# Splitting the two loads that follow stores in a DMA-fed batched matmul (a·bᵀ, fp32 in and out)

## Chip, core and metric

The kernel runs on one core of a Trainium2 chip. The metric is the device time of one launch in microseconds, given as the median of several runs. Shares and durations come from one further execution that the hardware profiler recorded.

## What is computed

```python
batch, m, k, n = 16, 512, 512, 512
a = randn(batch, m, k)   # float32
b = randn(batch, n, k)   # float32
out = matmul(a, b.transpose(0, 2, 1)).astype(float32)   # out[e] = a[e] @ b[e].T
```

Every operand is 16 x 512 x 512 float32, 16.78 MB. Two of them are read and one is written, 50.33 MB in all.

## The kernel before

**Work.** The sixteen batches are taken as eight pairs, `u` = 0 to 7. A load brings one operand of one pair: two batches, 1024 rows of 512 floats, 2 MB. It is laid over the 128 partitions so that each partition holds eight consecutive rows, which is one run of 16 KB in HBM for each partition. Loads are counted by `n_ld`: even ones are `a`, odd ones `b`, and load `n_ld` belongs to pair `n_ld // 2`. A store writes one batch of the output, 1 MB, four rows and so a run of 8 KB for each partition; stores are counted by `n_st`.

**Engines.** VectorE (DVE) casts each load into two bf16 halves (`ha`, `wa` or `hb`, `wb`, lines 167 to 175). TensorE (PE) transposes them (line 247) into PSUM tile `tp`. ScalarE (ACT) brings the transposed `a` back (`ta`, line 206) and VectorE the transposed `b` (`tb`, line 187). TensorE multiplies (line 266) into `ps`, and ScalarE copies the product into the output buffer `ob` (line 224).

**Buffers.** There are `NL` = 7 load slots and `NO` = 7 output slots. Load `n_ld` may be issued once the cast of load `n_ld` - 7 has gone far enough (`s_cd`). A store may be issued once its batch is in `ob` (`s_out`).

**Queue.** All loads, and all stores but the first, are issued by SyncE (SP) into one DMA queue, in an order written out by hand; the waits above are taken by SP in that order:

```python
ORDER = "LLLLLLLLLSSSLLLLLSSSLLSSSSSSSSS"
```

So nine loads (0 to 8) come first, then stores 1 to 3, loads 9 to 13, stores 4 to 6, loads 14 and 15, and stores 7 to 15. Store 0 is issued by GpSimd (POOL, line 135) into a queue of its own. The first two loads are already issued as two transfers of 1 MB each (lines 103 and 106), four rows and 8 KB for each partition, so that VectorE can begin early; all others are one transfer of 2 MB (line 110). Stores are issued on line 115.

**Who tells the engines that a load is there.** GpSimd walks the same `ORDER`. For each load it waits on the semaphore of the load's slot, `s_ld[slot]`, which grows by 16 when a transfer has landed, and then adds to `s_go`, on which VectorE waits. For the loads that are one transfer it adds 2 to `s_go` at once.

Of the kernel before, what the change touches and what calls it, by code (L numbers as in the profile page):

```python
# [10 lines left out]
def kernel(  # L11
# [6 lines left out]
    nc = tc.nc  # L18
# [3 lines left out]
    J = M // P  # L22
# [6 lines left out]
    NL = 7  # L29
# [5 lines left out]
    def sbuf(name, shape, dtype):  # L35
        return ctx.enter_context(nc.sbuf_tensor(name, shape, dtype))

    def sem(name):
        return tc.alloc_semaphore(name)

    with tc.tile_critical(no_gpsimd_drain=True):  # L41
        ident = sbuf("ident", [P, P], bf16)
        one = sbuf("one", [P, 1], f32)
        ld = sbuf("ld", [P, NL, 2 * J, K], f32)
# [10 lines left out]
        s_ld = [sem(f"s_ld{i}") for i in range(NL)]  # L55
        s_second = [sem(f"s_second{i}") for i in range(2)]
# [3 lines left out]
        def landed(n):  # L60
            return 16 * (n // NO + (n % NO > 0))
# [27 lines left out]

        n_ld, n_st = 0, 1
        for what in ORDER:
            if what == "L":
                u, slot = n_ld // 2, n_ld % NL
                src = (a if n_ld % 2 == 0 else b)[2 * u:2 * u + 2].rearrange(
                    "e (p j) k -> (e p) j k", j=2 * J
                )
                if n_ld >= NL:

                    nc.sync.wait_ge(s_cd, n_ld - NL + 2)
                if n_ld < 2:
                    nc.sync.dma_start(
                        ld[:, slot, :J, :], src[:, :J, :]
                    ).then_inc(s_ld[slot], 16)
                    nc.sync.dma_start(
                        ld[:, slot, J:, :], src[:, J:, :]
                    ).then_inc(s_second[slot], 16)
                else:
                    nc.sync.dma_start(ld[:, slot], src).then_inc(s_ld[slot], 16)  # L110
                n_ld += 1
            else:
                slot = n_st % NO
                nc.sync.wait_ge(s_out, n_st + 1)
                nc.sync.dma_start(
                    out[n_st].rearrange("(p j) n -> p j n", j=J), ob[:, slot]
                ).then_inc(s_st[slot], 16)
                n_st += 1
        for n in range(batch - NO, batch - 1):
            nc.sync.wait_ge(s_st[n % NO], landed(n))  # L120


        n_ld, n_st = 0, 1
        for what in ORDER:
            if what == "L":
                got = nc.gpsimd.wait_ge(s_ld[n_ld % NL], 16 * (n_ld // NL + 1))
                if n_ld < 2:
                    got.then_inc(s_go, 1)
                    nc.gpsimd.wait_ge(s_second[n_ld], 16).then_inc(s_go, 1)
                else:  # L130
                    got.then_inc(s_go, 2)
                n_ld += 1
                if n_ld == 4:
                    nc.gpsimd.wait_ge(s_out, 1)
                    nc.gpsimd.dma_start(  # L135
                        out[0].rearrange("(p j) n -> p j n", j=J), ob[:, 0]
                    ).then_inc(s_first, 16)
                elif n_ld == NL:
                    nc.gpsimd.wait_ge(s_first, 16).then_inc(s_of, 1)
            else:  # L140
                if n_st < batch - NO:
                    nc.gpsimd.wait_ge(
                        s_st[n_st % NO], landed(n_st)
                    ).then_inc(s_of, 1)
                n_st += 1
# [12 lines left out]
        with nc.Fori(0, pairs, engines=[dve]) as u:  # L158
            for x, (h, w, s_c, s_w) in enumerate(
                ((ha, wa, s_ca, s_wa), (hb, wb, s_cb, s_wb))  # L160
            ):
                src = ld[:, bass.ds((u * 2 + x) % NL, 1)].rearrange("p o j k -> p (o j) k")
# [148 lines left out]
```

## Time and profile before

| | |
|---|---|
| median of 5 runs | 126.8 us (126.28 to 127.26) |
| the profiled execution's own time | 127.23 us |
| its span, first to last instruction | 125.4 us |
| TensorE, VectorE, ScalarE busy | 73%, 56%, 54% of the span |
| DMA queue of SP (q1) | 49.29 MB, 93.8% of the 16 DMA engines' span |
| DMA queue of GpSimd (q0) | 1.05 MB, 2.0% |
| moved in all | 50.33 MB, 401 GB/s over the span |
| granted TensorE clock, mean | 0.953 |

A transfer runs on 16 DMA engines at once, each of which serves 8 of the 128 partitions; for each partition of a transfer there is one packet (16 KB for a whole load, 8 KB for a store), and each engine ends a transfer with a packet of 4 bytes that moves the semaphore. "Landing" is the time from the issue of a transfer to the last of the 16 semaphore steps. In the slices of the page each digit is a tenth of busy time in a fortieth of the span (3.14 us), and the row GB/s is what the DMA engines moved in it. The DMA share can read slightly over 1 in a short window, since a packet counts in the window where it begins.

### The profile page before, as it was taken

Reading aid. Unit: us, or ns where it says so; the run is one execution under the profiler, and the core shown is the slowest. Engines: PE = TensorE matmul, PEld = TensorE weight load, DVE = VectorE, ACT = ScalarE, POOL = GpSimd, SP = SyncE. Lnnn points to the kernel's source line nnn. Section 1 sums busy time; section 2 is a strip of 40 time slices with the busy share of each in tenths; the row PEclk is TensorE's granted clock in tenths of the full one; section 3 lists DMA queues with packets and bytes.
Section 4 is the critical chain, followed back from the end, with each engine's and each line's share of the span. In section 5 each row is a group of like instructions: output and inputs, shape, how many; then the busy total and the mean of one; then the engine's idle time right before and its main releaser. Section 6 shows DMA issues by size and latency. Waiting matters only on the chain. (4 is left out here: it accounts for less than half of the span.)

```text
span 125.4 us, 2407 instructions
## 1 busy us (share of the span) xinstructions
PE 91.6 (73%) x768; PEld 56.7 (45%) x768; DVE 70.1 (56%) x112; ACT 68.2 (54%) x130; POOL 1.7 (1%) x7
## 2 busy tenths in 40 slices
PE   0005299998998999899608999894989998994000
PEld 0005294477347646744408645741476457441000
DVE  0055679658867884792058894789058569400000
ACT  4005135589459567955820666934596669655000
POOL 2000000030000000000000000000000000000000
PEclk9999999999999999999995999999999999999655
DMA  4999999999999999999999999999999999999950
GB/s 94 400 431 444 444 418 423 428 423 381 408 449 423 418 428 421 423 434 431 402 423 423 444 439 428 413 418 428 434 418 449 389 428 421 434 423 423 428 251 10
DMA packets 4896, 50.33 MB, mean 401 GB/s; under 512 B 544, under 2 KB 544, under 8 KB 544
## 3 DMA queue, kind: packets, MB, share of 16 engines
q1 hardware_dynamic: 4752, 49.29, 93.8%
q0 software_dynamic: 144, 1.05, 2.0%
HBM read 33.55 MB, written 16.78 MB: 401 GB/s over the span
## 5 line engine op out<-in xcount | busy, mean ns | idle before, releaser
L266 PE MATMUL ps<-tb,ta 128*128 128x512 bf16 x256 | 58.0, 379 | 2.2 <-PEq L148 1.8
L224 ACT COPY ob<-ps 128x512 f32 x64 | 34.6, 588 | 27.2 <-PE ps L266 23.4
L206 ACT COPY ta<-tp 128x512 bf16<-128x512 bf16 x64 | 32.9, 604 | 18.8 <-PE tp L247 18.8
L266 PEld LDWEIGHTS ps<-tb,ta 128*128 128x128 bf16 x256 | 24.0, 97 | 32.7 <-issue 5.7
L247 PE MATMUL tp<-ident,ha 128*128 128x128 bf16 x256 | 19.9, 234 | 12.6 <-PEq L148 12.6
L247 PEld LDWEIGHTS tp<-ident,ha 128*128 128x128 bf16 x256 | 17.3, 106 | 15.9 <-issue 14.2
L247 PE MATMUL tp<-ident,hb 128*128 128x128 bf16 x256 | 18.5, 230 | 8.0 <-PEq L148 7.8
L187 DVE COPY tb<-tp 128x1024 bf16<-128x1024 bf16 x32 | 21.3, 685 | 4.2 <-DVEq L148 4.1
L247 PEld LDWEIGHTS tp<-ident,hb 128*128 128x128 bf16 x256 | 16.3, 104 | 8.7 <-issue 8.7
L167 DVE CAST hb<-ld 128x1024 bf16 x8 | 5.5, 694 | 13.9 <-DVEq L148 13.9
L182 DVE COPY ha<-wa 128x2048 bf16<-128x2048 bf16 x8 | 5.6, 694 | 10.9 <-DVEq L148 10.6
L167 DVE CAST ha<-ld 128x1024 bf16 x8 | 5.5, 687 | 6.5 <-DVEq L148 6.5
L172 DVE CAST hb<-ld 128x1024 bf16 x8 | 5.5, 687 | 1.1 <-DVEq L148 1.1
L172 DVE CAST ha<-ld 128x1024 bf16 x8 | 5.5, 688 | 1.0 <-DVEq L148 1.0
L186 DVE COPY hb<-wb 128x2048 bf16<-128x2048 bf16 x8 | 5.5, 686 | 0.5 <-DVEq L148 0.5
L175 DVE CAST wa<-ld 128x1024 bf16 x8 | 5.5, 686 | 0.0
L170 DVE CAST wb<-ld 128x1024 bf16 x8 | 5.5, 686 | 0.0
L170 DVE CAST wa<-ld 128x1024 bf16 x8 | 5.5, 686 | 0.0
L175 DVE CAST wb<-ld 128x1024 bf16 x8 | 5.5, 686 | 0.0
L197 ACT ACT_TABLE_LOAD x1 | 1.3, 1283 | 1.1 <-SPq L41 1.1
L135 POOL DMA_DIRECT2D out_dram<-ob x1 | 1.1, 1053 | 23.6 <-ACT ob L224 23.6
L83 POOL TENSOR_SCALAR_AFFINE_SELECT ident<-ident 128x128 bf16<-128x128 bf16 x1 | 0.3, 284 | 0.2 <-POOL ident L81 0.2
(6 smaller groups left out, 0.8 us busy)
## 6 DMA issues: line engine op xcount, KB each, us to landing
out_dram<-ob SPq DMA_DIRECT2D x15, 1024.0 KB, 22.2
ld<-in_a_dram SPq DMA_DIRECT2D x7, 2048.0 KB, 29.7
ld<-in_b_dram SPq DMA_DIRECT2D x7, 2048.0 KB, 33.6
ld<-in_a_dram SPq DMA_DIRECT2D x2, 1024.0 KB, 6.2
ld<-in_b_dram SPq DMA_DIRECT2D x2, 1024.0 KB, 10.2
out_dram<-ob POOLq DMA_DIRECT2D x1, 1024.0 KB, 13.1
```

The costliest lines, as they stand in the source:

```text
L167: nc.vector.tensor_copy(out=h[:, :J, :], in_=src[:, :J, :HK]).then_inc(s_cd, 1)
L170: nc.vector.tensor_copy(out=w[:, :J, :], in_=src[:, :J, HK:])
L172: nc.vector.tensor_copy(out=h[:, J:, :], in_=src[:, J:, :HK]).then_inc(s_c, 1)
L175: nc.vector.tensor_copy(out=w[:, J:, :], in_=src[:, J:, HK:]).then_inc(s_w, 1)
L182: nc.vector.tensor_copy(out=ha[:], in_=wa[:]).then_inc(s_ca, 1)
L186: nc.vector.tensor_copy(out=hb[:], in_=wb[:]).then_inc(s_cb, 1)
L187: nc.vector.tensor_copy(out=tb[:, ko, :], in_=tp[:, 2 + ko % 2].rearrange("k j p -> k (j p)"),).then_inc(s_eb, 1)
L197: nc.scalar.copy(out=one[:], in_=nc.const_aps.tensor(1.0, (P, 1), f32))
L206: c = nc.scalar.copy(out=ta[:, ko, e * J * P:(e + 1) * J * P].rearrange("k (j p h) -> k j p h", j=J, h=2), in_=tp[:, ko % 2, :, e * HP:(e ...
L224: c = nc.scalar.copy(out=dst[:, j, :].rearrange("m (p j) -> m p j", j=2 * J), in_=ps[:, j, :].rearrange("m (j p) -> m p j", j=2 * J),)
L247: t = nc.tensor.transpose(tp[:, 2 * x + g, j, :], h[:, j, g * P:(g + 1) * P], ident[:])
L266: t = nc.tensor.matmul(ps[:, j, :], ta[:, ko, (e * J + j) * P:(e * J + j + 1) * P], tb[:, ko, :].rearrange("k (j p) -> k j p", j=2 * J)[:, ...
```

## The change

A load that comes right after a store in `ORDER` is issued as two transfers instead of one: first the first four rows of each partition (a run of 8 KB), then the last four. By `ORDER` these are load 9 (`b` of pair 4, slot 2) and load 14 (`a` of pair 7, slot 0). Both transfers step the same semaphore `s_ld[slot]`; a list `count` holds what the semaphore must reach for each load, and GpSimd waits for that, so it still waits for the whole load. The data lands in the same places. On SP there are 33 rows of instructions instead of 31: two more DMA issues and nothing else. On the other engines the instructions and their order are the same; only line numbers move by 7.

```diff
+        parts = [0] * NL
+        count = []
+        last = None
         n_ld, n_st = 0, 1
         for what in ORDER:
             if what == "L":
...
-                if n_ld < 2:
+                if n_ld < 2 or last == "S":
                     nc.sync.dma_start(
                         ld[:, slot, :J, :], src[:, :J, :]
                     ).then_inc(s_ld[slot], 16)
-                    nc.sync.dma_start(
-                        ld[:, slot, J:, :], src[:, J:, :]
-                    ).then_inc(s_second[slot], 16)
+                    nc.sync.dma_start(ld[:, slot, J:, :], src[:, J:, :]).then_inc(
+                        s_second[slot] if n_ld < 2 else s_ld[slot], 16
+                    )
+                    parts[slot] += 1 if n_ld < 2 else 2
                 else:
                     nc.sync.dma_start(ld[:, slot], src).then_inc(s_ld[slot], 16)
+                    parts[slot] += 1
+                count.append(16 * parts[slot])
                 n_ld += 1
...
                 n_st += 1
+            last = what
...
-                got = nc.gpsimd.wait_ge(s_ld[n_ld % NL], 16 * (n_ld // NL + 1))
+                got = nc.gpsimd.wait_ge(s_ld[n_ld % NL], count[n_ld])
```

## Prediction

> **What bounds the kernel now.** I read the slices of the page first, for whether any resource is full the whole time.
>
> ```profile
> PE   0005299998998999899608999894989998994000
> ACT  4005135589459567955820666934596669655000
> DMA  4999999999999999999999999999999999999950
> GB/s 94 400 431 444 444 418 423 428 423 381 408 449 423 418 428 421 423 434 431 402 423 423 444 439 428 413 418 428 434 418 449 389 428 421 434 423 423 428 251 10
> q1 hardware_dynamic: 4752, 49.29, 93.8%
> ```
>
> The DMA row is at 9 from the second slice to the last but two, while PE and ACT have stopped two slices before. The 16 DMA engines are the bound: 50.33 MB at some 425 GB/s is 118 us of a span of 125.4. Next came the queue of SP and the transfers' landings, for whether the queue ever runs dry. The lines below are the timeline of SP from 38 to 60 us (start, duration, what), then the DMA issues of four short windows, one transfer each: store 3 (issued at 38.65), load 9 (39.03), load 14 (59.86) and the last store (115.25). The last column is issue to landing.
>
> ```profile
> 38.65 0.33 SPq L115 DMA_DIRECT2D out_dram<-ob  x1
> 39.03 0.43 SPq L110 DMA_DIRECT2D ld<-in_b_dram  x1
> ...
> 47.98 11.84 SPq L115 DMA_DIRECT2D out_dram<-ob  x3
> 59.86 0.53 SPq L110 DMA_DIRECT2D ld<-in_a_dram  x1
> ```
>
> ```profile
> out_dram<-ob SPq DMA_DIRECT2D x1, 1024.0 KB, 19.6
> ld<-in_b_dram SPq DMA_DIRECT2D x1, 2048.0 KB, 24.9
> ld<-in_a_dram SPq DMA_DIRECT2D x1, 2048.0 KB, 36.1
> out_dram<-ob SPq DMA_DIRECT2D x1, 1024.0 KB, 8.8
> ```
>
> Both loads that are to be split stand 25 to 36 us in the queue. Landings come in the order of issue, so the queue works off its transfers one after the other and is never empty. The last store is issued at 115.25 us and lands at 124.05, behind three transfers that are still under way: the end is set by the DMA engines and not by the last copy. So only what the engines lose counts, and the third view asks where they lose: the windows of 3 us around load 9, which follows store 3.
>
> ```profile
> 52.00:55.00 3.00, 1.00 1.01 423
> 55.00:58.00 3.00, 1.00 1.05 445
> 58.00:61.00 3.00, 1.00 1.00 382
> 61.00:64.00 3.00, 1.00 1.02 437
> ```
>
> (The columns are the granted clock, the DMA share and GB/s.) From 58 to 61 us the engines count as busy and yet move 382 GB/s: against 430, 0.33 us is lost, and it is lost just after the engines turned from stores to load 9 (at 56.9 to 57.7 us). The trace's own records of the packets say how. A 16 KB packet takes 611 ns, an 8 KB packet 309. Behind store 3 seven packets of load 9 take 995 to 1581 ns and one 744, on about half of the 16 engines, each the third or fourth packet after the turn; all are over by 60.5 us except the 744, and none of the packets of 62 to 80 us stands out. Behind store 6, at load 14, eight packets take 644 to 1585 ns, between 90.7 and 92.8 us. Averaged over the engines this is 0.34 and 0.18 us.
>
> An average isn't what ends the kernel, though: each engine has fixed partitions and so a fixed share of the bytes, and the slowest sets the end. By the landing events (median engine, last engine) store 3 ended at 57.87 and 58.21, load 9 at 62.46 and 63.90, load 14's predecessor at 89.45 and 91.08, load 14 at 94.21 and 95.95, load 15 at 99.10 and 101.17, the last store at 121.07 and 124.07. The last engine's lag grew by 1.10 us over load 9 (0.34 to 1.44), by 0.11 over load 14 (1.63 to 1.74) and by 0.33 over load 15 (to 2.07). So the stalls behind stores are worth up to 1.2 us at the end, 1.5 with load 15.
>
> **The change part by part.**
>
> *Smaller packets and two more transfers.* Load 9 and load 14 each go from 8 packets of 16 KB on each engine to 16 of 8 KB, and get one more closing packet of 9 ns. By the packet rows: 16 x 309 - 8 x 611 + 9 = 65 ns for a load. The landings of the first loads give the other bound, since those are halves already: the second, the fourth and the first whole load land at 8.57, 13.54 and 18.43 us, so two halves took 4.97 us and one whole load 4.89, a difference of 0.08. I take 0.08, the row that holds all of it: +0.16 us for both (0.13 by the lower). It lies on the path that sets the end, since every engine works both loads off before the last store.
>
> The Trainium skill speaks against the change here. Its page "DMA: Bandwidth & Descriptors", section "Anatomy of one DMA — SWDGE (gpsimd) path", fits a fixed 2.0 us for a DMA beside its bytes; two more DMAs would by that be +4.0 us, an estimate. That fit is of single transfers issued from GpSimd, and the row of 0.08 us for transfers that queue behind each other from SP decides against it.
>
> *Two more issues on SP.* An issue takes 0.33 to 0.53 us on SP's row. Behind the added half of load 9 stand loads 10 and 11, which go out 0.45 us later and whose turn comes over 20 us later: hidden. Issues at 47.98 and 50.16 us took 0.82 and 1.0 us, with ten and eleven transfers outstanding; one more could hold SP longer there, up to the next landing (50.6 us). SP's next issue is due at 59.49, so 8 us of cover remain; without it the cost would be some 0.5 us of SP's time, which no engine of the DMA would feel while transfers are queued. Behind the added half of load 14 SP next issues load 15 at 64.97, 4.6 us later: hidden.
>
> *The wait of GpSimd.* It still waits for the whole load, once, and adds 2 to `s_go`. No cast starts earlier. VectorE waits 7.11 us for load 9 (its cast starts at 64.24, the load lands at 63.90), so it would see 0.08 us of delay at once; the stores of that pair are issued at 76 and 79 us and take their turn in the queue after 101: hidden. The last load lands at 101.17, and 14.1 us later the last store is issued, 3 us before the first engine comes to its end of the store ahead (118.23): that is the cover of the compute side, 3 us.
>
> *The stall behind the stores.* No row shows a load in 8 KB runs behind a store, so it is bounded from both sides. If the stall belongs to the 16 KB packets, it goes: -1.2 us at the end, -1.5 with load 15. The nearest row of 8 KB packets at the start of reading is the kernel's own start: there 8 KB packets take up to 1439 ns too, several engines have their longest in the second or third packet (1439, 1275, 1000), and the engines lose 0.68 us on average before 6 us, where the 16 KB load behind store 3 lost 0.34. Part of that is the first latency, which a queue behind stores hides. So the start of reading stalls with 8 KB packets as well, at about the same packet time and the same place, and I take the stall as unchanged, 0. For the other end, the same row could mean twice the loss: +1.1 us at load 9, +0.1 at load 14.
>
> *Sum.* +0.16 + 0 = +0.16 us. The profiled execution of 127.23 us (span 125.4 and 1.83 around it) would become 127.39. It lay 0.43 us above the median; taken to the median, 126.8 + 0.16 gives 127.0 us.
>
> **The rivals.**
>
> *The stall goes (faster).* For it: stalls stand at just those two loads and not in the 16 KB loads of 62 to 80 us, and an engine that meets a store's 8 KB packets and a load's 16 KB packets in one window is what the change takes away. Against: the start of the kernel. Worth -1.2 to -1.5 + 0.16, so -1.0 to -1.3 us: 125.5 to 125.8. The engines next behind the slowest end at 122.6, so the room is there. If half the stall goes, -0.6 + 0.16 is -0.4: 126.4, which no measurement tells from no change.
>
> *The start of reading stalls more in 8 KB runs (slower).* Place: the first microseconds of load 9 and 14 behind stores 3 and 6, on the engine that is last already. Price: by the start of the kernel up to twice the present loss, +1.2 + 0.16 = +1.4 us, 128.2; half of that gives 127.6. It decides from 0.47 us of added stall on the last engine on. For it: 0.68 against 0.34 us. Against: the three halves behind the first one landed 2.49 us apart, without a stall.
>
> *The change does nothing to the order of the data.* As far as the packet time goes this is my forecast; it can't do less, since two more issues stand on SP.
>
> **How the numbers follow.** A measurement of this kernel can tell about 0.5%, 0.63 us, from no change: 126.17 to 127.43 counts as the same. Unchanged stall: 0.40, at 127.0, itself 126.5 to 127.4, since the runs shown spread by half a microsecond to either side. Stall gone by more than half: 0.30, 125.5 to 126.1. Half gone: 0.05, 126.4. Stall grown by over 0.47 us: 0.25, 127.5 to 128.2. So faster 0.30, same 0.45, slower 0.25. The range leaves out about a third of the faster case and a third of the slower one: 125.7 to 127.9.
>
> **What would show it right or wrong.** Right: 5184 packets in place of 4896 (256 more of data, 32 closing); loads 9 and 14 in 309 ns packets; still some packets of 700 to 1200 ns longer than that within 3 us behind store 3 and store 6; a window at 58 to 61 us near 380 GB/s; a lag of the last engine of 1 us or more after load 9. The forecast is wrong, and the kernel faster, if that window holds 425 GB/s and the last engine lands load 9 within 0.5 us of the median; it is wrong the other way if the lag after load 9 is over 1.9 us. If the last store lands later than 115.25 + 8.8 by more than the lag explains, a term is missing.

## The result and the profile after

The change moved nothing that can be measured. Over all runs the changed kernel has a median of 126.73 us (42 runs) and the kernel before 126.89 us (79 runs); the ratio is 0.9994 with a 95% interval of 0.9983 to 1.0005, which is -0.22 to +0.06 us. The forecast was no change that can be measured, 127.0 us, within 125.7 to 127.9. The profiled execution took 127.01 us with a span of 125.2 us.

The page of the changed kernel: the digits of DMA activity in 40 slices, GB/s in the same slices, the packets, and SP's queue with its packets, MB and share of 16 engines.

```profile
DMA  3999999999999999999999999999999999999970
GB/s 81 406 432 440 432 434 429 419 424 395 400 450 429 429 424 414 427 421 416 427 434 429 440 419 440 416 416 424 427 387 437 416 416 434 421 429 427 421 304 13
DMA packets 5184, 50.33 MB, mean 402 GB/s; under 512 B 576, under 2 KB 576, under 8 KB 576
q1 hardware_dynamic: 5040, 49.29, 94.1%
```

The packets are the 288 more that were forecast (SP's queue has 5040, 144 to a transfer, so SP issues 35 transfers where it issued 33), and the DMA engines are still the bound. The timeline of SP for 39 to 70 us (start, duration, line, what) shows the two added issues and a side effect of them:

```profile
39.36 0.33 SPq L121 DMA_DIRECT2D out_dram<-ob  x1
39.74 0.43 SPq L106 DMA_DIRECT2D ld<-in_b_dram  x1
40.21 0.43 SPq L109 DMA_DIRECT2D ld<-in_b_dram  x1
...
44.56 1.07 SPq L114 DMA_DIRECT2D ld<-in_a_dram  x1
46.97 1.70 SPq L114 DMA_DIRECT2D ld<-in_b_dram  x1
...
60.58 0.44 SPq L106 DMA_DIRECT2D ld<-in_a_dram  x1
61.07 0.44 SPq L109 DMA_DIRECT2D ld<-in_a_dram  x1
64.92 4.46 SPq L114 DMA_DIRECT2D ld<-in_b_dram  x1
```

Issues that follow took up to 4.46 us where 0.33 to 0.53 was usual, with more transfers outstanding. Nobody waited for them: load 15, issued at 64.92, landed at 100.94.

The windows of 3 us around the two turns from stores to loads, in the changed kernel (granted clock, DMA share, GB/s):

```profile
55.00:58.00 3.00, 1.00 1.02 429
58.00:61.00 3.00, 1.00 1.00 391
61.00:64.00 3.00, 1.00 1.06 451
89.00:92.00 3.00, 1.00 1.03 393
92.00:95.00 3.00, 1.00 1.03 423
```

The same two windows of the second turn in the kernel before:

```profile
89.00:92.00 3.00, 1.00 1.05 423
92.00:95.00 3.00, 1.00 1.00 426
```

From 58 to 61 us the engines move 391 GB/s in 8 KB packets, where they moved 382 in 16 KB packets: the dip stays. Behind store 6 it is deeper than before, 393 GB/s where it was 423. In the packet records ten packets behind store 3 and thirteen behind store 6 are over 100 ns longer than 309, up to 1247 and 1248 ns; only one of the ten and two of the thirteen are the 700 ns longer that the prediction named as a sign. On the average engine this is 0.25 and 0.38 us lost, 0.63 in all; before it was 0.34 and 0.18, 0.52 in all. By the landing events (median and last engine) store 3 ended at 57.81 and 58.48, load 9 at 62.47 and 63.85, the last store at 121.44 and 123.86. So the last engine's lag grew by 0.71 us over load 9, before by 1.10, and the whole ended 0.21 us sooner in this pair of executions, which is within the spread of the runs.

### The profile page after: what moved, and what is told of

The parts are those of the page before. It is cut to its first block, busy times and chain, and to the rows that moved or that the text cites. A ratio compares the mean times of both kernels' runs of the same rounds, so it can differ in the third digit from the quotient of the medians.

```text
span 125.2 us, 2409 instructions
## 1 busy us (share of the span) xinstructions
PE 92.6 (74%) x768; PEld 57.8 (46%) x768; DVE 70.1 (56%) x112; ACT 68.2 (54%) x130; POOL 1.4 (1%) x7
## 3 DMA queue, kind: packets, MB, share of 16 engines
q1 hardware_dynamic: 5040, 49.29, 94.1%
## 5 line engine op out<-in xcount | busy, mean ns | idle before, releaser
L254 PE MATMUL tp<-ident,hb 128*128 128x128 bf16 x256 | 19.3, 235 | 7.1 <-PEq L155 7.1
L254 PEld LDWEIGHTS tp<-ident,hb 128*128 128x128 bf16 x256 | 17.2, 107 | 7.6 <-issue 7.4
```

The source lines that it names most:

```text
L254: t = nc.tensor.transpose(tp[:, 2 * x + g, j, :], h[:, j, g * P:(g + 1) * P], ident[:])
```

## The experiments

Two theories stood against each other. T: the stall belongs to the turn from stores to loads whatever the length of the runs, a split costs 0.08 us of the DMA engines, and the slowest engine sets the end. R: the stall belongs to the 16 KB packets. Every kernel was timed beside the kernel before, twelve runs each (seven of the first). "Long" below means over 100 ns more than a packet of that size takes otherwise. A loss is all the time that the packets in the few microseconds behind a turn take beyond the usual 611, 309 or 156 ns, as a mean over the 16 engines; with the long packets alone it comes out up to 0.16 us lower, most of all for 4 KB packets.

**Every load in halves.** The condition `if n_ld < 2 or last == "S":` of the changed kernel became:

```diff
-                if n_ld < 2 or last == "S":
+                if True:
```

> All sixteen loads go as two transfers in 8 KB runs: 14 more splits than the kernel before, 12 more than the changed one. Theory T (a split costs 0.08 us of the DMA engines' time and the stall belongs to the turn from stores to loads, whatever the run): 14 x 0.08 = +1.1 us, ratio to the kernel before 1.009; long packets still only in the 3 us behind the two turns. Rival P (more transfers cost nothing that can be measured, since the stall is a bit smaller in 8 KB runs): 1.000 to 1.003. Rival R (8 KB runs have no stall): ratio 1.000 or less and no long packets behind the turns.

Measured: ratio 1.0085 (1.0053 to 1.0118), +1.08 us (+0.67 to +1.50). The page counts the packets:

```profile
DMA packets 6912, 50.33 MB, mean 399 GB/s; under 512 B 768, under 2 KB 768, under 8 KB 768
```

1.08 us over 14 splits is 0.077 us each (0.048 to 0.107 by the interval), the size that was read from the first loads of the kernel before. The stalls stayed behind the two turns: 0.42 us behind store 3 and 0.18 behind store 6, with 8 KB packets throughout; here SP's issues took up to 6.4 us, and the price of the packets alone still accounts for the time. P and R fall.

**Quarters.** The two loads behind stores as four transfers each, runs of 4 KB (against the changed kernel):

```diff
-                    nc.sync.dma_start(ld[:, slot, :J, :], src[:, :J, :]) ...
-                    nc.sync.dma_start(ld[:, slot, J:, :], src[:, J:, :]) ...
+                    step = J if n_ld < 2 else J // 2
+                    for j in range(0, 2 * J, step):
+                        nc.sync.dma_start(
+                            ld[:, slot, j:j + step, :], src[:, j:j + step, :]
+                        ).then_inc(s_second[slot] if n_ld < 2 and j else s_ld[slot], 16)
...
```

> Loads 9 and 14 go as four transfers each, in runs of 4 KB: 6 transfers more than the kernel before. Theory T (the stall does not ask for the run; what is paid is the packets): a 4 KB packet at half of an 8 KB one plus some 4 ns, so 8 x (4 x 158 - 611) + 27 = 0.2 us for a load, +0.4 us in all, ratio 1.001 to 1.005, and long packets behind both turns of 0.2 to 0.4 us on the average engine. Rival R (smaller runs weaken the stall): less than 0.1 us of long packets behind each turn, ratio under 0.999.

Measured: ratio 1.0028 (1.0004 to 1.0053), +0.36 us (+0.05 to +0.67). A 4 KB packet took 156 to 160 ns. The losses behind the turns were 0.30 and 0.32 us, in long packets alone 0.20 and 0.17. The stall stayed in 4 KB runs, above R's mark of 0.1, and the time fits the price of the packets.

**VectorE told of the first half.** Loads 9 and 14 in halves, the second half on a semaphore of its own (against the kernel before; the last two lines stand in SP's loop and in GpSimd's):

```diff
-        s_second = [sem(f"s_second{i}") for i in range(2)]
+        s_second = {i: sem(f"s_second{i}") for i in (0, 1, 9, 14)}
...
-                if n_ld < 2:
+                if n_ld in s_second:
```

> Loads 9 and 14 in halves as in the changed kernel, but the second half has a semaphore of its own and VectorE is told of the first half when it lands, 2.5 us ahead of the second. Theory T (the end is set by the DMA engines, the compute has 3 us of cover): VectorE starts pair 4 some 2 us earlier, the time stays, ratio 0.997 to 1.003. Rival V (the changed kernel gains nothing only because VectorE still waits for the whole load): 1 to 2 us faster, ratio 0.985 to 0.993.

Measured: ratio 1.0005 (0.9980 to 1.0030). VectorE's timeline, first of this kernel and then of the changed one (start, duration, line, what, the idle time before and what ended it):

```profile
62.70 0.69 DVE L167 CAST hb<-ld 128x1024 bf16 x1 [4.70 <-DVEq L148]
63.31 0.69 DVE L170 CAST wb<-ld 128x1024 bf16 x1
65.12 0.69 DVE L172 CAST hb<-ld 128x1024 bf16 x1 [1.12 <-DVEq L148]
```

```profile
64.20 0.69 DVE L174 CAST hb<-ld 128x1024 bf16 x1 [6.35 <-DVEq L155]
64.81 0.69 DVE L177 CAST wb<-ld 128x1024 bf16 x1
65.41 0.69 DVE L179 CAST hb<-ld 128x1024 bf16 x1
```

The cast began 1.5 us sooner, after 4.70 us of waiting in place of 6.35, then waited 1.12 us for the second half, and the time stayed. The earlier cast did not make the product earlier in this execution: the second half landed at 64.84 us, where the whole load had landed at 63.85, and the pair's two stores were issued at 77.08 and 79.26 us, in the changed kernel at 76.87 and 79.05. Over the twelve runs telling VectorE early bought nothing, so the wait of GpSimd for the whole load is not where a gain went. In this execution the stall behind store 3 was the longest of all with this order, 0.55 us, and the one behind store 6 0.07: the size changes from one execution to the next.

**Four turns in place of two,** whole loads:

```diff
-    ORDER = "LLLLLLLLLSSSLLLLLSSSLLSSSSSSSSS"
+    ORDER = "LLLLLLLLLSSLSLLLLSSLSLSSSSSSSSS"
```

> Whole loads as before; the order on SP is 9 loads, 2 stores, 1 load, 1 store, 4 loads, 2 stores, 1 load, 1 store, 1 load, 9 stores: four turns from stores to loads in place of two, same bytes and packets. Theory T: four clusters of long packets, each 0.2 to 0.35 us on the average engine: 0.4 to 0.7 us more on the average engine, ratio 1.003 to 1.010. Rival S: two clusters, ratio 1.000.

Measured: ratio 1.0029 (1.0004 to 1.0055), +0.37 us (+0.05 to +0.70). Windows of the first, second, third and fourth turn (two each for the first, the third and the fourth; clock, DMA share and GB/s, the clock being TensorE's):

```profile
52.00:55.00 3.00, 1.00 1.04 437
55.00:58.00 3.00, 1.00 1.01 355
63.00:66.00 3.00, 1.00 1.02 418
87.00:90.00 3.00, 0.50 1.06 415
90.00:93.00 3.00, 0.50 0.92 380
94.00:97.00 3.00, 1.00 1.02 434
97.00:100.00 3.00, 1.00 0.99 423
```

Three turns lost 0.58, 0.13 and 0.37 us; the fourth lost nothing. The first and the third stand behind two stores each, the second and the fourth behind a single one. So a turn mostly costs, but not always, and T's four clusters were one too many. The last store was issued at 118.09 us and not at 115.25, and the engines that were ahead ran dry before the last two stores. The last engine did not: it landed the last three stores 2.46 and 2.49 us apart, in the kernel before 2.47 and 2.48. So the added time does not show there.

**Store 0 from SP,** behind load 8 and ahead of store 1:

```diff
-    ORDER = "LLLLLLLLLSSSLLLLLSSSLLSSSSSSSSS"
+    ORDER = "LLLLLLLLLSSSSLLLLLSSSLLSSSSSSSSS"
...
-                if n_ld == 4:
-                    nc.gpsimd.wait_ge(s_out, 1)
-                    nc.gpsimd.dma_start(...).then_inc(s_first, 16)
```

> Store 0 is issued by SP behind load 8, ahead of store 1, and not by GpSimd; nothing else changes. In the kernel before, load packets are long from 27 to 34 us, while that store runs beside loads: 0.6 us on the average engine. Theory T (reads lose time where writes run beside or just ahead of them): these long packets go, the two clusters behind the turns stay, and the kernel is 0.3 to 0.6 us faster, ratio 0.995 to 0.998. Rival U (that loss is caught up later, since it only moves the engines against each other): ratio 1.000.

Measured: ratio 1.0001 (0.9977 to 1.0025). Windows of this kernel, and then the same of the kernel before:

```profile
27.00:30.00 3.00, 1.00 1.03 437
30.00:33.00 3.00, 1.00 1.03 437
...
42.00:45.00 3.00, 1.00 0.99 421
45.00:48.00 3.00, 1.00 0.97 371
```

```profile
27.00:30.00 3.00, 1.00 1.04 382
30.00:33.00 3.00, 1.00 1.00 410
...
42.00:45.00 3.00, 1.00 1.02 437
45.00:48.00 3.00, 1.00 1.01 431
```

The loss at 27 to 33 us went, but 0.31 us came back at 45.4 to 46.9 us, inside load 8, before the first store packet of the run (47.0 us) and with no store ahead of it. T is wrong in that a turn isn't needed for long load packets, and the gain it forecast did not come. The ratio is the one that U forecast; that the loss is caught up later, as U has it, no row shows.

**One turn.** First with 11 loads ahead of it, then with 12:

```diff
-    ORDER = "LLLLLLLLLSSSLLLLLSSSLLSSSSSSSSS"
+    ORDER = "LLLLLLLLLLLSSSSSSLLLLLSSSSSSSSS"   # e2_one_turn
+    ORDER = "LLLLLLLLLLLLSSSSSSLLLLSSSSSSSSS"   # e7_one_turn_12
```

> Whole loads as before; the order on SP is 11 loads, 6 stores, 5 loads, 9 stores, so there is one turn from stores to loads in place of two; bytes and packets are the same. Theory T: only one cluster of long packets, and one stall less: 0.2 us on the average engine and 0.1 to 1.1 us on the last one, so 0 to 1 us faster, ratio 0.992 to 1.000. Rival S (the stall belongs to a time or a place in memory, not to the turn): two clusters remain, ratio 1.000. If the compute falls behind for the later stores, slower, and then the queue of SP runs dry near the end.

Measured with 11: ratio 0.9996 (0.9969 to 1.0023). One cluster of long packets, 0.13 us, and store 13 landed at 118.62 us where it had landed at 119.12. But the windows near the end show the queue run dry:

```profile
114.00:117.00 3.00, 1.00 0.64 268
117.00:120.00 3.00, 1.00 0.77 314
```

The last store was issued at 119.31 us, 4.06 us later than before, and landed 4.3 us after its issue: the end now waits for the last pair's product. What that wait costs this trace doesn't show, since the last store landed at 123.57 us where it had landed at 124.07, as much sooner as store 13; over all runs the time is the same. With 12 loads ahead, pair 5 has both operands before the turn:

> Whole loads as before; the order on SP is 12 loads, 6 stores, 4 loads, 9 stores: one turn from stores to loads, as with 11 loads ahead of it, but load 11 (b of pair 5) comes ahead of the turn, so that pair 5 needn't wait for it and the last store should be issued near 116 us and not at 119. Theory T (one stall less, and the engines don't run dry at the end): 0.3 to 1.0 us faster than the kernel before, ratio 0.992 to 0.998, last engine's lag at the last store 2.7 us or less. Rival W (the lag of the last engine grows in the stores whatever comes before, so the stall is not worth its size at the end): ratio 0.998 to 1.001.

Measured with 12: ratio 0.9981 (0.9955 to 1.0006). One cluster, 0.24 us; the last store was issued at 117.07 us, the last engine's lag at it was 2.42 us where it had been 3.00. Once more, for the interval:

> The order of 12 loads, 6 stores, 4 loads, 9 stores once more, for its interval. Theory T: as in the first runs, ratio 0.996 to 0.999, one cluster of long packets behind store 6 and none behind loads. Rival W (the first ratio of 0.998 was chance): 0.999 to 1.002.

Measured: ratio 0.9976 (0.9960 to 0.9991), 0.30 us faster (0.11 to 0.51); one cluster of 0.34 us, and no long packets from the 55th to the 64th microsecond. This version beats the kernel before by a little. The last store is issued at 117.51 us, 2.26 us later than before, and its line of the DMA issues (the last column is issue to landing) shows that it still stands behind others:

```profile
out_dram<-ob SPq DMA_DIRECT2D x1, 1024.0 KB, 6.5
```

It landed at 123.99 us, where it had landed at 124.07, so there is less cover than before. That the gain comes from the missing turn would fit, but no trace separates it. Against the changed kernel it was not timed in pairs, only each against the kernel before.

**The changed kernel again,** on that same chip:

> The changed kernel once more on the same chip as the order with one turn. Theory T: ratio 1.000 to 1.002, two clusters of long 8 KB packets, behind stores 3 and 6, 0.15 to 0.45 us each on the average engine. Rival R (the run size weakens the stall): clusters under 0.15 us.

Measured: ratio 0.9997 (0.9973 to 1.0021). The losses were 0.26 us behind store 3 and 0.06 behind store 6, the second under what T expected and by itself within R's mark. The window behind store 3:

```profile
58.00:61.00 3.00, 1.00 0.99 382
```

That is the 382 GB/s of the kernel before, with packets of half the size.

## Why the prediction was right, and where not

*The bound.* The end is set by the DMA engines as the prediction read it. 14 more transfers for the same bytes showed at their full price, and SP's longer issues did not. With 12 loads ahead of the one turn the last store was issued 2.26 us later than before, and the kernel was no slower for it.

*The price of a split.* Taken as 0.08 us from the landings of the first loads; 0.077 us (0.048 to 0.107) when it was paid 14 times. This term is shown. The fixed 2.0 us for a DMA in the Trainium skill (page "DMA: Bandwidth & Descriptors", section "Anatomy of one DMA — SWDGE (gpsimd) path") would have made 28 us of those 14, an estimate. The 1.08 us measured decides, for transfers queued behind each other from SP.

*The stall.* Taken as unchanged, between -1.5 and +1.2 us. In halves the loss on the average engine behind store 3 was 0.25, 0.26, 0.55 and 0.42 us, behind store 6 0.38, 0.06, 0.07 and 0.18 (the changed kernel twice, the early start, all halves); in whole loads with the same two turns 0.34 and 0.32, 0.18 and 0.44 (before, store 0 from SP). The means are 0.27 us of eight in halves and 0.32 of four in whole loads, and one execution differs from the next by more than that. Both rivals fall: the stall neither went nor doubled. The time says the same: had half of the stall gone from the end, the sum would be -0.4 us, below the interval.

*The sum.* It was +0.16 us, and the interval of -0.22 to +0.06 us lies below it, by 0.1 us at its upper end. By the interval of the price two splits cost 0.10 to 0.21 us, so something between 0.03 and 0.43 us stands against them. The stall, taken as unchanged, is the term without a size of its own, and a stall on the last engine that is a little smaller in 8 KB runs would do. The traces don't show one: the last engine's lag grew over load 9 by 0.71, 0.84, 1.43 and 0.79 us in halves, 0.94 in the mean, and by 1.10 and 0.59 in whole loads, 0.85 in the mean. So the point stays open. That the time came out this near to no change is partly luck, since what stands against the price has about its size.

*The cover.* One line of the forecast was that more transfers outstanding could hold SP for longer, hidden by 8 us. Issues of 1.07 to 4.46 us came, more than the 0.5 us that was reckoned, and were hidden by transfers that stood 20 to 36 us in the queue.

*What was read wrongly behind it* is the name of the stall. The prediction tied it to the turn from stores to loads. Three runs speak for the turn: with one turn there is one cluster, with four there are three, and in every run with turns after stores 3 and 6 the largest loss from 35 us on stands behind one of them. Store 0 from SP speaks against it as the only cause, and the fourth turn without loss against it as a sufficient one. With one turn load 9 had no long packets, nor had any load from 57 to 62 us, so neither the place in memory nor the time alone makes them. What does was not settled.

## What to carry to other kernels

Where a queue is full all the time, as here, a transfer more costs its packets and not a latency: price it by the landings of a small and a large transfer that follow each other in the same trace, and multiply it by a dozen when the price is to be seen. A stall that shows on half of the DMA engines is worth what it adds to the last engine, and that is to be followed through the landing of each transfer, not read from the mean. Before shortening packets to cure a stall, look whether the same stall stands where packets are already short: here the first loads of the same trace did.

## What the runs showed of the hardware that was not expected

The issue of a DMA on SP, 0.33 us in most places, took 1.07 to 4.46 us in the changed kernel, up to 6.40 with all loads in halves and 6.95 in the run that told VectorE early. In all eleven traces no issue on SP took over 0.9 us with eight or fewer transfers outstanding; the longer ones had nine to twelve.

Load packets went long before any store packet ran: at 45.4 us in the run with store 0 from SP, where the first store packet ran at 47.0, and in the kernel before from 27.6 us on, two microseconds ahead of the first packet of GpSimd's store (29.7 us). All eleven traces have this: load packets go long 0.9 to 2.1 us ahead of the first store packet of the execution. Ahead of later stores, away from the turns, at most three load packets did. So the first store of a run is worth a test of its own; none was made.

The end of the kernel is the end of one engine: in the kernel before, the last engine landed the last store 3.00 us behind the median and 1.4 us behind the next engine. Its lag grows in the stores after load 15 whatever went before: from 2.07 to 3.00 us there, from 1.54 to 2.42 in the changed kernel, and from 1.81 to 2.82 (up to store 13) in the second runs with one turn. The packets show how: in the kernel before, between 102.9 and 116 us, 36 store packets of 8 KB, nearly all one behind the other and so on one engine, took 313 to 366 ns in place of 309, 0.71 us together. No experiment was aimed at that part.
